# A two-layer decoder trunk on one core: ones matmuls ahead of the first weights, full-width norm sums, outputs on two queues

## The chip, the cores and the metric

The kernel runs on one core of a Trainium2 chip. A core has a matrix engine (TensorE, "PE" in the profile, with its weight loads as "PEld"), a vector engine (VectorE, "DVE"), an activation engine (ScalarE, "ACT"), GpSimd ("POOL") and SyncE ("SP"), which here only issues transfers. SyncE and ScalarE each have a queue of transfers; 16 DMA engines carry them out. The engines run their own instruction streams in order and wait for one another by semaphores. The metric is the device time of one execution in microseconds.

## The reference

Input is x with 256 positions of 2048 features, all in fp32. Each of two layers does:

```
h = rms_norm(x); z = h @ w_in[l]                 # 2048 -> 5120
q, k, v, gu, gv = split(z)                       # 8 heads of 128, 8 gMLP groups of 128
attn = dilated_attention(rotary(q), rotary(k), v)
gm   = gelu(gu) * (tril(w_s) @ layer_norm(gelu(gv)) + b_s)
x = x + concat(attn, gm) @ w_out[l]              # 2048 -> 2048
x = x + square(relu(rms_norm(x) @ w_up[l])) @ w_down[l]   # 2048 -> 8192 -> 2048
```

A last `rms_norm(x, final_g)` follows. `rms_norm` is x times the reciprocal root of (mean of squares + 1e-6), times a gain per feature.

## The kernel before

**Layout.** x stays on chip as 16 chunks of 128 features (partitions) by 256 positions, in the tile `x`. The host hands every weight matrix over in blocks of 128 x 1024 (512 KB), in the order of use.

**Matmuls.** fp32 values are split into a high part (type fp32r, a copy by ScalarE) and a low part (the rest, a subtraction by VectorE), for weights (`hi`, `lo`, lines 118 and 126) and for activations (`hs`, lines 181 and 182). Each product is three matmuls: high by high, low weight by high, high weight by low. `natural` (lines 275 to 294) puts positions on the output's partitions and is used for v and gv; one block is 12 matmuls of 512 columns. `transposed` (lines 242 to 273) puts features there; one block is 24 matmuls of 256 columns, 12 for each of two output chunks, which share one PSUM bank `acc`. Smaller matmuls (scores, transposes, norms) are plain fp32 into banks `aux`.

**Order.** All work is written out by hand as a list of steps, one for each block of weights. Before the matmuls of a step the loop (lines 623 to 642) issues what later blocks need: high parts up to some blocks ahead, then low parts, then the loads of raw weights on SyncE's queue; six raw blocks, seven high and six low ones fit. After a step come its consumer, functions hooked to that step's number, and a queue of attention work. Engines run their instructions in this written order.

**The start** (lines 612 to 621). The gains (`cols`) are issued on ScalarE's queue; ScalarE runs one Tanh, which brings in its function table. SyncE issues x's first two chunks, the first weight block in two halves, the next two chunks of x, the second block, and so on. ScalarE makes the high parts of chunks 0 and 1, then the two high halves of the first block; VectorE the low parts in the same order. The first step is a `natural` one: its matmuls want, in turn, the high weight half, the low weight half, and the low part of chunk 0.

**Norms.** The reciprocal root is applied after the matmul, since it is one number for a position. `square` gathers squares over chunks in the tile `nacc` (the last pair of the last norm stays alone, in `nsq`); `factor` (lines 201 to 209) sums them over partitions with matmuls that use the squares as weights and a column of ones, so that positions land on partitions in a tile of two columns; `rsqrt` (lines 220 to 237) takes the reciprocal root there by a bit trick and three Newton rounds, twelve VectorE instructions; `spread` (lines 210 to 218) brings the row of roots to all partitions with two matmuls by the identity. For the norm ahead of the MLP (`n2`) `factor` is hooked behind the MLP's second step and `spread` behind its third; the first reader is the consumer of the fourth step (line 563).

**The tail.** The last `w_down` steps end with `update` (lines 326 to 337): VectorE adds the result to x, ScalarE squares, and in the last layer ScalarE multiplies x by the final gain. After the last step come `factor`, `spread` without its copy, and for each of eight pairs of chunks a VectorE product with the row of roots, read from PSUM, and a transfer of 256 KB on SyncE's queue (lines 646 to 652).

Of the kernel before, what the change touches and what calls it, by code (L numbers as in the profile page):

```python
# [21 lines left out]
F32 = mybir.dt.float32  # L22
# [3 lines left out]
OP = mybir.AluOpType  # L26
# [25 lines left out]
BUDGET = 1.2  # L52
D_SCORES, D_NORM, D_TURN, D_VALUES = 2, 1, 3, 2
# [21 lines left out]
def trunk(ctx: ExitStack, tc: tile.TileContext, layout, xT, consts, gains, w, b_sp, w_sp, out):  # L75
# [59 lines left out]
    ones = cp.tile([P, P], F32, name="ones")  # L135
    x = cp.tile([P, KC, S], F32, name="x")
# [35 lines left out]
    class Norm:  # L172
# [37 lines left out]
        def spread(self, copy=True):  # L210
            self.ps = aux_bank()
            for tt in range(2):
                pe.matmul(self.ps[:, tt * P:(tt + 1) * P], lhsT=self.r[:, tt:tt + 1].to_broadcast([P, P]), rhs=ident,
                          start=(tt == 0), stop=True, skip_group_check=True)
            if not copy:
                return
            self.R = t32("nR", [S])
            act.activation(self.R, self.ps[:, 0:S], AF.Copy)

    def rsqrt(e, y, src, scale, eps, shape):  # L220

        tag = "x".join(map(str, shape))
        v = t32("rv", shape, tag=f"rv{tag}")
        t = t32("rt", shape, tag=f"rt{tag}")
        vec.tensor_scalar(v, src, scale, eps, op0=OP.mult, op1=OP.add)
        vec.tensor_scalar(t.bitcast(I32), v.bitcast(I32), 1, None, op0=OP.logical_shift_right)
        e.tensor_scalar(y.bitcast(I32), t.bitcast(I32), -1.0, MAGIC, op0=OP.mult, op1=OP.add)
        for _ in range(3):
            if e is vec:
                vec.scalar_tensor_tensor(t, y, -0.5, y, op0=OP.mult, op1=OP.mult)  # L230
                vec.tensor_tensor(t, t, v, op=OP.mult)
                vec.scalar_tensor_tensor(y, t, 1.5, y, op0=OP.add, op1=OP.mult)
# [9 lines left out]
    def transposed(name, l, row0, nk, col0, ncols, moving, after, between=None):  # L242
# [10 lines left out]
        for n, (c, k0) in enumerate(order):  # L253
# [4 lines left out]
            def mm(wt=wt, k0=k0, c=c):  # L258
                if k0 == 0:
                    accs[c] = acc_bank()  # L260
                ps = accs[c]
                for cb in range(2):
                    o = ps[:, cb * S:(cb + 1) * S]
                    for k in range(4):
# [3 lines left out]
                        pe.matmul(o, lhsT=hi, rhs=xs[:, 0, :], start=(k0 + k == 0 and cb == 0), stop=False,  # L268
# [57 lines left out]
    def update(norm, c, ps, final, last):  # L326

        alone = last and c == KC - 2
        for j in range(2) if alone else [slice(0, 2)]:
            xj = x[:, c + j, :] if alone else x[:, c:c + 2, :]  # L330
            vec.tensor_tensor(xj, xj, pair(ps)[:, j, :], op=OP.add)  # L331
# [7 lines left out]
    def layer(l, n1, n2, n3, last):  # L339
# [229 lines left out]
        for e in range(9):  # L569
            if e < 8:  # L570
                transposed("w_up", l, 0, KC, e * 1024, 1024, from_hs, after_up(e))
            if e:
                transposed("w_down", l, (e - 1) * 1024, 8, 0, D, from_tiles([hid[e - 1]], NH),
                           lambda c, ps, e=e: update(n3, c // P, ps, e == 8, last))
        hook(base + 1, n2.factor)
        hook(base + 2, n2.spread)
# [35 lines left out]
    nc.scalar.dma_start(cols, gains)  # L612
    vec.memset(ones, 1.0)
    warm = cp.tile([P, 1], F32, name="warm")
    act.activation(warm, ones[:, 0:1], AF.Tanh)
# [31 lines left out]
    n.factor()  # L647
    n.spread(copy=False)
    ov = out.rearrange("(k p) t -> p k t", p=P)
    for c in range(0, KC, 2):  # L650
        vec.tensor_tensor(x[:, c:c + 2, :], x[:, c:c + 2, :], n.ps[:, None, 0:S].to_broadcast([P, 2, S]), op=OP.mult)  # L651
        nc.sync.dma_start(ov[:, c:c + 2, :], x[:, c:c + 2, :])
# [36 lines left out]
```

## Time and profile before

| | us |
|---|---|
| median of 3 runs (2075.73 to 2076.0) | 2075.97 |
| the profiled execution | 2075.94 |
| its span | 2073.8 |
| TensorE busy | 2056.3 |
| VectorE busy | 1254.5 |
| ScalarE busy | 930.1 |
| GpSimd busy | 68.3 |

The span runs from the first recorded instruction to the last; the execution's own time has some 2 us more around it. In rows of the timeline stand start, duration, engine, line, operation, what is written and read, the count, and the idle time before it with what ended it. In rows of the chain of waits stand start, length and the work that held up what came next. In rows of grouped instructions stand count, busy time, the mean duration in ns, and the idle time before. A row for a window has the busy time of each engine, then granted TensorE clock, DMA share and GB/s. Times inside the profile count from the span's start.

### The profile page before, as it was taken

How to read it: one execution, taken by the hardware profiler on the slowest of the kernel's cores; microseconds unless marked ns; L12 is line 12 of the kernel's file. 1: busy time of each engine (PE TensorE's matmuls, PEld its weight loads, DVE VectorE, ACT ScalarE, POOL GpSimd, SP SyncE). 2: the span in 40 equal slices, each digit the busy share in tenths (PEclk: the TensorE clock that was granted, in tenths of full speed). 3: DMA queues.
4: the chain of work that ended last, by engine and by line, in shares of the span. 5: the costliest groups of instructions: out<-in, count | busy, mean ns of one | idle time of the engine just before them, and what ended most of it. 6: DMA issues, size and time to landing. Idle time of an engine off the chain costs nothing.

```text
span 2073.8 us, 40168 instructions
## 1 busy us (share of the span) xinstructions
PE 2056.3 (99%) x17212; PEld 2019.2 (97%) x17212; DVE 1254.5 (60%) x1502; ACT 930.1 (45%) x1128; POOL 68.3 (3%) x90
## 2 busy tenths in 40 slices
PE   8999999999999999999999999999999999999997
PEld 7998999999999999999989989999999999999997
DVE  7566766656565655655756666665565555555555
ACT  6555444344343443434545554543344434434333
POOL 0002300000000000000000032000000000000000
PEclk9999999999999999999999999999999999999998
DMA  8544555555565556655564455555655656556562
GB/s 309 190 163 165 189 191 188 203 192 186 192 204 192 194 184 203 197 188 202 187 215 162 164 183 183 194 182 204 204 183 186 202 199 200 187 186 201 189 201 82
DMA packets 111523, 395.36 MB, mean 191 GB/s; under 512 B 12272, under 2 KB 16368, under 8 KB 111344
## 3 DMA queue, kind: packets, MB, share of 16 engines
q1 hardware_dynamic: 110480, 390.12, 56.5%
q8 instruction: 134, 2.20, 0.4%
q10 hardware_dynamic: 864, 2.68, 0.3%
q14 instruction: 45, 0.37, 0.1%
HBM read 390.65 MB, written 2.10 MB: 189 GB/s over the span
## 4 chain that ended last, share of the span: by engine, by line
PE 99%; DVE 0%; DMA 0%; ACT 0%; issue 0%; DVEq 0%; ACTq 0%
PE acc L268 29%; PE acc L270 29%; PE acc L272 29%; PE acc L291 3%; PE acc L293 3%; PE acc L292 3%; PE aux L505 0%; PE aux L449 0%; PE aux L409 0%; PE aux L438 0%; DVE x L651 0%; PE aux L206 0%; PE aux L412 0%; PE aux L451 0%; PE aux L359 0%; DMA x<-in_xT 0%
## 5 line engine op out<-in xcount | busy, mean ns | idle before, releaser
L118 ACT ACTIVATE hi<-raw 128x1024 fp32r<-128x1024 f32 (+1 forms) x737 | 754.9, 1053 | 455.4 <-PE acc L272 374.9
L126 DVE TENSOR_TENSOR lo<-raw,hi 128x1024 fp32r<-128x1024 f32 (+1 forms) x737 | 864.2, 1218 | 54.2 <-ACT hi L118 26.3
L268 PE MATMUL acc<-hs,hi 128*128 128x256 f32 x2816 | 781.5, 278 | 0.0
L272 PE MATMUL acc<-hs,hi 128*128 128x256 f32 x2816 | 778.8, 277 | 0.0
L270 PE MATMUL acc<-hs,lo 128*128 128x256 f32 x2816 | 778.8, 277 | 0.0
L268 PE MATMUL acc<-half,hi 128*128 128x256 f32 x2560 | 706.7, 276 | 0.0
L272 PE MATMUL acc<-half,hi 128*128 128x256 f32 x2560 | 706.6, 276 | 0.0
L270 PE MATMUL acc<-half,lo 128*128 128x256 f32 x2560 | 706.6, 276 | 0.0
L268 PEld LDWEIGHTS acc<-hs,hi 128*128 128x128 f32 x2816 | 529.9, 188 | 0.4 <-issue 0.2
L270 PEld LDWEIGHTS acc<-hs,lo 128*128 128x128 f32 x2816 | 528.8, 188 | 0.4 <-issue 0.2
L272 PEld LDWEIGHTS acc<-hs,hi 128*128 128x128 f32 x2816 | 528.6, 188 | 0.0
L270 PEld LDWEIGHTS acc<-half,lo 128*128 128x128 f32 x2560 | 480.6, 188 | 0.0
L268 PEld LDWEIGHTS acc<-half,hi 128*128 128x128 f32 x2560 | 480.6, 188 | 0.0
L272 PEld LDWEIGHTS acc<-half,hi 128*128 128x128 f32 x2560 | 480.6, 188 | 0.0
L331 DVE TENSOR_TENSOR x<-x,acc 128x512 f32<-128x512 f32 (+1 forms) x152 | 99.6, 660 | 319.2 <-PE acc L272 319.2
L459 ACT ACTIVATE half<-mz 128x512 fp32r<-128x512 f32 x64 | 40.6, 634 | 364.6 <-DVE mz L564 364.6
L563 DVE TENSOR_TENSOR mz<-acc,nR 128x512 f32<-128x512 f32 x64 | 44.3, 692 | 230.7 <-PE acc L272 230.7
L291 PE MATMUL acc<-hi,hs 128*128 128x512 f32 x256 | 102.8, 402 | 5.4 <-ACT hi L118 5.4
L293 PE MATMUL acc<-hi,hs 128*128 128x512 f32 x256 | 101.3, 396 | 0.0
L292 PE MATMUL acc<-lo,hs 128*128 128x512 f32 x256 | 100.9, 394 | 0.0
L181 ACT ACTIVATE hs<-x,cols 128x256 fp32r<-128x256 f32 x64 | 29.1, 501 | 96.4 <-DVE x L331 94.8
L460 DVE TENSOR_TENSOR half<-mz,half 128x512 fp32r<-128x512 f32 x64 | 44.3, 692 | 44.8 <-ACT half L459 44.8
(90 smaller groups left out, 680.2 us busy)
## 6 DMA issues: line engine op xcount, KB each, us to landing
raw<-in_w SPq DMA_DIRECT2D x735, 512.0 KB, 4.4
x<-in_xT SPq DMA_DIRECT2D x8, 256.0 KB, 7.3
out<-x SPq DMA_DIRECT2D x8, 256.0 KB, 3.0
spb<-in_b_sp ACTq DMA_DIRECT2D x2, 512.0 KB, 7.3
wsp<-in_w_sp ACTq DMA_DIRECT2D x2, 512.0 KB, 9.0
raw<-in_w SPq DMA_DIRECT2D x2, 256.0 KB, 4.0
con<-in_consts ACTq DMA_DIRECT2D x1, 512.0 KB, 6.6
cols<-in_gains ACTq DMA_DIRECT2D x1, 56.0 KB, 2.9
```

The costliest lines, as they stand in the source:

```text
L118: act.activation(self.h[:, j * m:(j + 1) * m], self.raw[:, j * m:(j + 1) * m], AF.Copy)
L126: vec.tensor_tensor(lo[:, r], self.raw[:, r], self.h[:, r].bitcast(F32), op=OP.subtract)
L268: pe.matmul(o, lhsT=hi, rhs=xs[:, 0, :], start=(k0 + k == 0 and cb == 0), stop=False, skip_group_check=True)
L270: pe.matmul(o, lhsT=wt.lo[:, k, cb * P:(cb + 1) * P], rhs=xs[:, 0, :], start=False, stop=False, skip_group_check=True)
L272: pe.matmul(o, lhsT=hi, rhs=xs[:, 1, :], start=False, stop=last, skip_group_check=True)
L291: pe.matmul(ps, lhsT=xh, rhs=hi, start=(k0 + k == 0), stop=False)
L292: pe.matmul(ps, lhsT=xh, rhs=lo, start=False, stop=False)
L293: pe.matmul(ps, lhsT=xl, rhs=hi, start=False, stop=(k0 + k == KC - 1))
L331: vec.tensor_tensor(xj, xj, pair(ps)[:, j, :], op=OP.add)
L459: act.activation(t[:, c:c + 2, 0, :], src, AF.Copy)
L460: vec.tensor_tensor(t[:, c:c + 2, 1, :], src, t[:, c:c + 2, 0, :].bitcast(F32), op=OP.subtract)
L563: vec.tensor_tensor(z, pair(ps), n2.R[:, None, :].to_broadcast([P, 2, S]), op=OP.mult)
```

## The change

*Start.* x's first two chunks go on ScalarE's queue, followed there by the gains; all other loads stay on SyncE's. The second weight block is loaded, and both first blocks are split, in two halves. Nine fp32 matmuls of ones by ones into a spare bank are written ahead of all other TensorE work. The parts of the first chunks are interleaved with those of the weights: chunk 0, both high halves, chunk 1, both low halves, and the same for the second block.

*Norm ahead of the MLP.* `factor` and `spread` give way to `everywhere`: two fp32 matmuls with a full matrix of ones as weights leave the sum on all partitions, and `rsqrt` runs on 128 x 256.

*Last norm.* The last block of the last `w_down` writes its two chunks to two banks, so that the add of the first can begin ahead of the second's matmuls. Four matmuls on ones sum the squares; ScalarE takes a root with Sqrt (its table is asked for by a small Sqrt early in the last MLP), VectorE a reciprocal and one Newton round, and writes the row of roots to PSUM; ScalarE copies it to SBUF for GpSimd.

*Outputs.* GpSimd makes the pairs 10 and 14, VectorE the other six; transfers go alternately on SyncE's and ScalarE's queue.

```
+WARM = 9
@@ Norm
+        def total(self, n0, n1, last):
+            if n0 == 0:
+                self.ps = aux_bank()
+            parts = [a[:, j, :] for a in self.acc for j in range(2)]
+            for n in range(n0, n1):
+                pe.matmul(self.ps[:, 0:S], lhsT=ones, rhs=parts[n], start=(n == 0), stop=(last and n == n1 - 1))
+
+        def everywhere(self):
+            self.total(0, 2, True)
+            self.R = t32("nR", [S])
+            rsqrt(vec, self.R, self.ps[:, 0:S], 1.0 / D, NORM_EPS, [S], tags=("p0", "q"))
+
+        def finish(self):
+            y, v, t = t32("ny", [S], tag="p0"), t32("nv", [S], tag="q"), t32("nt", [S], tag="p1")
+            act.activation(y, self.ps[:, 0:S], AF.Sqrt, bias=eps, scale=1.0 / D)
+            vec.tensor_scalar(v, self.ps[:, 0:S], 1.0 / D, NORM_EPS, op0=OP.mult, op1=OP.add)
+            vec.reciprocal(y, y)
+            vec.scalar_tensor_tensor(t, y, -0.5, y, op0=OP.mult, op1=OP.mult)
+            vec.tensor_tensor(t, t, v, op=OP.mult)
+            vec.scalar_tensor_tensor(self.ps[:, S:2 * S], t, 1.5, y, op0=OP.add, op1=OP.mult)
+            self.R = t32("nR", [S])
+            act.activation(self.R, self.ps[:, S:2 * S], AF.Copy)
@@ transposed (apart: the last block has a bank for each chunk)
+                two = apart and c == ncols - 256
-                    accs[c] = acc_bank()
+                    accs[c] = [acc_bank(), acc_bank()] if two else acc_bank()
-                    o = ps[:, cb * S:(cb + 1) * S]
+                    o = ps[cb][:, 0:S] if two else ps[:, cb * S:(cb + 1) * S]
@@ update
-        alone = last and c == KC - 2
+        alone = last and final and c == KC - 2
-            vec.tensor_tensor(xj, xj, pair(ps)[:, j, :], op=OP.add)
+            vec.tensor_tensor(xj, xj, ps[j][:, 0:S] if alone else pair(ps)[:, j, :], op=OP.add)
@@ layer, MLP
-        hook(base + 1, n2.factor)
-        hook(base + 2, n2.spread)
+        hook(base + 1, n2.everywhere)
+        if last:
+            hook(base + 4, lambda: act.activation(warm, ones[:, 0:1], AF.Sqrt))
@@ load_to
-                nc.sync.dma_start(x[:, c:c + 2, :], xv[:, c:c + 2, :])
+                (nc.scalar if c == 0 else nc.sync).dma_start(x[:, c:c + 2, :], xv[:, c:c + 2, :])
+            if c == 0:
+                nc.scalar.dma_start(cols, gains)
@@ start
-    nc.scalar.dma_start(cols, gains)
     vec.memset(ones, 1.0)
+    vec.memset(eps, NORM_EPS)
+    spare = aux_bank()
+    for _ in range(WARM):
+        pe.matmul(spare[:, 0:P], lhsT=ones, rhs=ones, start=True, stop=True)
+    for i in range(RAW_BUFS):
+        load_to(i + 1, 2 if i < 2 else 1)
     act.activation(warm, ones[:, 0:1], AF.Tanh)
-    for i in range(RAW_BUFS):
-        load_to(i + 1, 2 if i == 0 else 1)
     for i in range(2):
-        norms[0].chunks(2 * i)
-        high_to(i + 1, 2 - i)
-        low_to(i + 1, 2 - i)
+        norms[0].chunks(2 * i, 1)
+        high_to(i + 1, 2)
+        norms[0].chunks(2 * i + 1, 1)
+        low_to(i + 1, 2)
@@ tail
-    n.factor()
-    n.spread(copy=False)
+    n.total(0, 4, True)
+    n.finish()
-    for c in range(0, KC, 2):
-        vec.tensor_tensor(x[:, c:c + 2, :], x[:, c:c + 2, :], n.ps[:, None, 0:S].to_broadcast([P, 2, S]), op=OP.mult)
-        nc.sync.dma_start(ov[:, c:c + 2, :], x[:, c:c + 2, :])
+    def scale(c):
+        e, r = (nc.gpsimd, n.R) if c in (10, 14) else (vec, n.ps[:, S:2 * S])
+        e.tensor_tensor(x[:, c:c + 2, :], x[:, c:c + 2, :], r[:, None, :].to_broadcast([P, 2, S]), op=OP.mult)
+
+    for i, c in enumerate((0, 2, 4, 10, 6, 8, 12, 14)):
+        scale(c)
+        (nc.sync if i % 2 == 0 else nc.scalar).dma_start(ov[:, c:c + 2, :], x[:, c:c + 2, :])
```

More of the change, by code (lines that the diff above doesn't have):

```diff
@@ L135, in trunk @@
     ones = cp.tile([P, P], F32, name="ones")
+    eps = cp.tile([P, 1], F32, name="eps")
+    warm = cp.tile([P, 1], F32, name="warm")
     x = cp.tile([P, KC, S], F32, name="x")
@@ L209, in factor, with spread @@
             rsqrt(vec, self.r, ps[:, 0:2], 1.0 / D, NORM_EPS, [2])
-        def spread(self, copy=True):
+        def spread(self):
             self.ps = aux_bank()
@@ L240, in trunk, with transposed @@
     steps = []
-    def transposed(name, l, row0, nk, col0, ncols, moving, after, between=None):
+    def transposed(name, l, row0, nk, col0, ncols, moving, after, between=None, apart=False):
         order = [(c, k) for c in range(0, ncols, 256) for k in range(0, nk, 4)]
@@ L267, in mm @@
                         last = k0 + k == nk - 1
-                        pe.matmul(o, lhsT=hi, rhs=xs[:, 0, :], start=(k0 + k == 0 and cb == 0), stop=False,
+                        pe.matmul(o, lhsT=hi, rhs=xs[:, 0, :], start=(k0 + k == 0 and (two or cb == 0)), stop=False,
                                   skip_group_check=True)
```

12 lines of the change are left out of this document (5 added, 7 removed).

## The prediction

> **What bounds the kernel now.** I read the page first, the busy times and the chain of waits, then the chain in order of time at both ends, because 99% of it lies on one engine.
>
> ```profile
> span 2073.8 us, 40168 instructions
> PE 2056.3 (99%) x17212; PEld 2019.2 (97%) x17212; DVE 1254.5 (60%) x1502; ACT 930.1 (45%) x1128; POOL 68.3 (3%) x90
> ...
> PE 99%; DVE 0%; DMA 0%; ACT 0%; issue 0%; DVEq 0%; ACTq 0%
> ```
>
> TensorE sets the end. The change leaves its projection matmuls as they are, so only three places can move: the first 11 us, the norm before each MLP (there TensorE itself does other work), and what follows the last projection matmul. The start, in the chain:
>
> ```profile
> 0.74 3.12 DMA x<-in_xT
> ...
> 3.95 0.91 ACT hs L181 x2
> ...
> 5.43 0.79 PE acc L291
> ...
> 9.93 0.43 PE acc L291
> 10.36 0.26 PE acc L292
> 10.62 0.23 PE acc L293
> ```
>
> Until about 10.3 us a matmul takes 0.43 us of the chain, afterwards 0.23: TensorE runs at half speed for its first 4.9 us, although the granted clock of the windows (below) reads 1.00 there. The first block of weights (12 matmuls) ends at 10.85.
>
> The tail, in the chain:
>
> ```profile
> 2058.52 0.13 PE acc L272
> ...
> 2058.67 0.43 DVE x L331
> ...
> 2059.12 0.42 ACT nsq L189
> ...
> 2059.59 1.07 PE aux L206 x8
> ...
> 2060.68 0.17 DVE rv L225
> ...
> 2063.06 1.24 PE aux L213 x4
> ...
> 2064.32 0.69 DVE x L651
> ```
>
> From the last projection matmul (2058.65) to the first scaled pair of chunks (2065.01) pass 6.4 us: residual add, square, sum over partitions into two columns, twelve tiny VectorE steps at 0.198 us each (2060.68 to 2063.06), a matmul pair that spreads the root, the first product. Then only transfers are left:
>
> ```profile
> 2065.04 5.02 SPq L652 DMA_DIRECT2D out<-x  x8
> ```
> ```profile
> 3.00:4.00 1.00, 0.00 (x0) 0.00 (x0) 0.00 (x0) 0.05 (x1) 0.00 (x0) 1.00 1.05 388
> ...
> 2061.00:2062.00 1.00, 0.00 (x0) 0.00 (x0) 0.83 (x6) 0.00 (x0) 0.00 (x0) 0.85 0.02 8
> ...
> 2066.00:2068.00 2.00, 0.00 (x0) 0.00 (x0) 2.00 (x5) 0.00 (x0) 0.00 (x0) 0.50 1.01 341
> ```
>
> In the windows (the last three columns are granted clock, DMA share, GB/s; the first row is from the loads at the start) the 16 engines are full at 341 GB/s while the outputs leave; eight of 256 KB are 2.1 MB, 6.2 us, plus about 2.5 us of start and landing, is the 8.76 us from first issue to the end of the span. VectorE and the issues pace a pair at 0.63 us (5.02 / 8), the engines take 0.77 for one.
>
> **Part 1: the tail.** Prices:
>
> ```profile
> L331 DVE TENSOR_TENSOR x<-x,acc 128x256 f32<-128x256 f32 x16 | 6.0, 418 | 20.7 <-PE acc L272 20.7
> L409 PE MATMUL aux<-k,q 128*128 128x256 f32 x32 | 8.2, 378 | 0.0
> L218 ACT ACTIVATE nR<-aux 128x256 f32<-128x256 f32 x4 | 1.5, 383 | 14.0 <-PE aux L213 14.0
> L427 DVE RECIPROCAL den<-den 128x4 f32<-128x4 f32 x8 | 1.4, 178 | 0.2
> L232 DVE SCALAR_TENSOR_TENSOR nr<-rt,nr 128x2 f32<-128x2 f32 x15 | 2.4, 161 | 0.5
> L351 POOL TENSOR_TENSOR wsp<-wsp,con 128x1024 f32<-128x1024 f32 x2 | 5.3, 2630 | 842.5 <-DMA wsp<-in_w_sp 842.5
> L615 ACT ACT_TABLE_LOAD x1 | 1.3, 1283 | 1.2 <-PEq L672 1.2
> ```
> ```profile
> 2059.78 0.89 ACT L199 ACTIVATE x<-x,cols 128x256 f32<-128x256 f32 x2
> ```
> ```profile
> 82.53 0.86 PE aux L409 x4
> ...
> 341.11 0.79 PE aux L206 x8
> ...
> 344.83 0.44 PE aux L213 x4
> ```
>
> An fp32 matmul leaves two records (L409 issues 16 and has 32), so 256 columns cost 0.43 (0.86 / 2).
>
> *Two banks for the last pair.* The add of chunk 14 no longer waits for the twelve matmuls of chunk 15 (12 x 0.114 = 1.4 us). Only chunk 15 stays on the path: add 2058.67 to 2059.10, square to 2059.54.
>
> *The sum.* Four fp32 matmuls of 256 columns in order: two on the accumulator and one on chunk 14 end at 2058.65 + 1.29 = 2059.94, later than the square; the fourth at 2060.37, its end 0.16 later (378 against a spacing of 215 ns): 2060.53. This takes the place of L206's end at 2060.66, and no spread follows.
>
> *The root.* ScalarE is in order: behind the square stand two gain multiplies (L199, 0.89 us) until 2060.4, just hidden by the sum. Sqrt by L218: 2060.55 to 2060.95. VectorE's mean-plus-eps runs beside it. Then four VectorE steps in a row on 256 columns (reciprocal, three of Newton). By L331 one is 0.42, with the 0.037 between dependent steps (0.198 against L232's 0.161) 0.46. The reciprocal is unseen at this width: at four columns it takes 178 ns where other steps take 161. If those 17 ns are fixed, it is 0.46; if they are per column (4.2 ns each), 256 columns cost 0.42 + 1.08 = 1.5. I take 0.46, since the only row says little more than "one more VectorE step", and keep 1.5 for the range. Root done at 2060.95 + 4 x 0.46 = 2062.8, first product at 2063.5, first output 2063.52. Gain 1.52; with the dear reciprocal 0.48.
>
> [...]
>
> *The outputs.* Two queues feed the same full engines: 0. The second queue's issue is hidden by the 0.77 us that each transfer takes. If a second queue let the engines write at the 388 GB/s of the loads, 2.1 MB would take 0.75 us less (range). GpSimd's two pairs, at half of L351 about 1.3 us each, start when ScalarE's copy of the root is there (2063.2), so pair 10 is ready at 2064.5 and pair 14 at 2065.8; the engines want them as fourth and last, at 2066.9 or later. Without that cover one of them late costs 0.5.
>
> *The table.* Tanh, Exp, Square and Copy all run on the one table load of 1.28 us. Sqrt is new; its load is asked for early in the last MLP, where ScalarE is under half busy and weights are prepared four blocks (11 us) ahead: 0. If Square or Copy needed the old table back, a load would fall between the last square and Sqrt: 1.3.
>
> **Part 2: the MLP norm, twice.** On TensorE the factor (0.79) and spread (0.44) give way to two fp32 matmuls of 256 columns (0.86): gain 0.37 each, 0.74 in all, straight off the path. VectorE now does twelve steps at 0.46 instead of 0.2, 3.1 us more, and the ScalarE copy goes. Behind the first of these steps, which waits for the sum, VectorE has the low halves of weights; they are made about five blocks ahead (13.7 us), and the four accumulator banks hold three groups back. VectorE is 60% busy, so it catches up: 0; uncovered it would be 3.1 us each.
>
> **Part 3: the start.** Rows of VectorE and ScalarE there:
>
> ```profile
> 0.73 0.45 ACTq L612 DMA_DIRECT2D cols<-in_gains  x1
> ...
> 4.49 0.88 DVE L182 SCALAR_TENSOR_TENSOR hs<-x,cols,hs 128x256 fp32r<-128x256 f32 x2 [3.49 <-ACT hs L181]
> 4.76 0.61 ACT L118 ACTIVATE hi<-raw 128x512 fp32r<-128x512 f32 x1
> ...
> 5.41 0.69 DVE L126 TENSOR_TENSOR lo<-raw,hi 128x512 fp32r<-128x512 f32 x1
> ...
> 6.60 0.63 ACT L118 ACTIVATE hi<-raw 128x512 fp32r<-128x512 f32 x1 [1.22 <-DMA raw<-in_w]
> ...
> 8.59 1.06 ACT L118 ACTIVATE hi<-raw 128x1024 fp32r<-128x1024 f32 x1 [0.41 <-DMA raw<-in_w]
> ...
> 11.73 1.23 DVE L126 TENSOR_TENSOR lo<-raw,hi 128x1024 fp32r<-128x1024 f32 x1
> ...
> 13.82 0.39 PE L292 MATMUL acc<-lo,hs 128*128 128x512 f32 x1
> ```
> ```profile
> cols<-in_gains ACTq DMA_DIRECT2D x1, 56.0 KB, 2.9
> ```
>
> If nine fp32 matmuls on ones (two passes of 128 columns, 0.11 us warm by L213, twice that slow: 9 x 0.44 = 4 us, about 1.1 to 5.1) bring the clock up, the first block shrinks from 5.4 us to 12 x 0.23 = 2.8. But operands set that stage then, and the new order makes them later. ScalarE now has hs 0, both high halves, then hs 1; VectorE has hs-low 0, hs-low 1, then the low halves. So the first low half, which the second matmul needs, waits for hs-low 1, that for hs 1, that for the second high half, that for its weights. From the time T at which x and the gains are there: 0.46 + 0.61 + 0.61 + 0.46 + 0.44 + 0.69 = T + 3.27, against T + 2.15 now (3.95 to 6.10).
>
> T itself: x and then the gains go on ScalarE's queue, the gains issued at 1.18 instead of 0.73. Lower bound 1.18 + 2.9 (their landing time now, 0.73 to about 3.6) = 4.1; upper, if x shares the engines with both 256 KB weight halves ahead of it, 3.86 + 512 KB / 388 GB/s = 5.2, with the gains 5.4. I take 4.7. The second block's weights come in two transfers instead of one, an issue more on SyncE (0.4), which runs ahead of the engines: 0. The second matmul then starts at 8.0, the second block at 10.5; its weights still land near 8.59, so high half 9.2, hs 3 9.65, hs-low 3 10.1, low halves 10.8 and 11.5, two more hs-lows and the third block's low part at 13.6. The third block's second matmul goes at 13.6 instead of 13.82: gain 0.2. If the second weight half lands at 6.6 as now, the second matmul waits until 8.8 and the third block is 0.45 later than now. I take 0 between them. Even with no such stall the third block's low part was ready only at 12.96 (11.73 + 1.23): the start can gain at most 13.82 - 12.96 = 0.9.
>
> **The sum.** 2075.94 (the profiled execution's own time, 2073.8 of span and 2.1 around it) - 1.52 - 0.74 - 0 = 2073.7. Its own time stands 0.03 below the median of 2075.97, so the forecast against that is the same.
>
> **Rivals.**
>
> *The clock is lost again: slower.* At the tail the granted clock falls from 1 to 0.5 inside the row 2061 to 2062 (mean 0.85, so near 2061.7), 3 us after the last projection matmul, though one-column matmuls ran until 2060.65; and at the start 4.9 us of matmuls passed before the speed rose (5.43 to about 10.3). In the new start TensorE has one real matmul between about 5.1 and 8.0. If the clock isn't raised by then, or is lost in this gap, the slow 4.9 us begin anew at the second matmul. At 8.0 they last to 12.9 and cover 11.4 matmuls; the other 11.6 up to the third block end at 15.6 instead of 13.6 (13.82 - 0.23): loss 2.0. With the late weight half they last from 8.8 to 13.7, and the third block begins at 16.4: loss 2.8, 2076.5. It decides the sign from a loss above 2.26, that is, if the second matmul comes after 8.3. Against it: the matmuls on ones are four microseconds of full work.
>
> [...]
>
> *The dear reciprocal:* 1.04 less gain, 2074.7. For it the 17 ns, against it that they may be fixed.
>
> *The start gains all that operands allow:* 0.9 more, 2072.8, if low halves come earlier than the written order says.
>
> *The outputs leave faster on two queues:* 0.75 more, 2072.9; against it stands the DMA share of 1.01.
>
> *A table load before Sqrt:* 2075.0.
>
> **How the numbers follow.** The forecast 0.42, the dear reciprocal 0.20, the clock 0.20, the start 0.08, the outputs 0.05, the table 0.05. Range: the two best cases reach 2072.8 and 2072.9, together 2072.0; the lost clock reaches 2076.5, with the dear reciprocal 2077.5. I take 2072.2 to 2076.6. A measurement of this kernel tells about 0.2% (4.2 us) from no change, and every case lies inside that: the gains together (1.52 + 0.74 + 0.9 + 0.75 = 3.9) don't reach it, nor do the losses together (1.04 + 2.8 + 1.3 = 5.1, less the 2.26). So same 0.94, and 0.03 on each side for what I haven't seen.
>
> **What would show it.** The first output issue 8.76 us before the end and about 1.5 us nearer to the last projection matmul than now; one VectorE reciprocal of 0.42 us, or of 1.5; the MLP norms' two matmuls at 0.86; the second real matmul at 8 to 8.8 us, released by the low half, and spacings of 0.23 from there. Wrong I am if the second matmul starts before 7, if spacings of 0.43 are seen past 11 us, or if the output phase is shorter than 8 us.

## The result, and the profile after

The changed kernel takes 2130.01 us (median of 5 runs, 2129.28 to 2130.41), the kernel before in the same series 2075.75 (2075.58 to 2076.0): a ratio of 1.0261 [1.0249, 1.0272]. It is 54 us slower where 2.3 us less was forecast. The profiled execution took 2130.33 us itself.

The page of the changed kernel, busy times:

```profile
span 2128.5 us, 40136 instructions
...
PE 2111.1 (99%) x17202; PEld 2073.3 (97%) x17202; DVE 1260.0 (59%) x1488; ACT 930.3 (44%) x1131; POOL 70.4 (3%) x92
```

TensorE still sets the end and is busy 55 us longer, with ten matmul records fewer. It isn't waiting either. These are all the waits of TensorE in the changed kernel (what waited, for whom; us in total, times, longest):

```profile
PE acc L321 <- ACT hi L119: 1.3, 1, 1.3
PE acc L322 <- DVE lo L127: 1.2, 1, 1.2
PE aux L649 <- DVE eps L646: 1.1, 1, 1.1
```

3.6 us, all at the start. The 55 us must lie in the matmuls themselves. Windows of 200 us inside the two MLPs, first of the kernel before, then of the changed one (length and sum; busy time and records of TensorE, its weight loads, VectorE, ScalarE, GpSimd; granted clock, DMA share, GB/s):

```profile
400.00:600.00 200.00, 200.00 (x1767) 200.00 (x1766) 115.11 (x120) 79.75 (x83) 0.00 (x0) 1.00 0.59 196
1600.00:1800.00 200.00, 200.00 (x1767) 200.00 (x1766) 115.56 (x123) 80.50 (x84) 0.00 (x0) 1.00 0.58 195
```
```profile
400.00:600.00 200.00, 200.00 (x1700) 200.00 (x1699) 110.74 (x116) 75.95 (x79) 0.00 (x0) 1.00 0.58 190
1600.00:1800.00 200.00, 200.00 (x1700) 200.00 (x1699) 111.46 (x116) 77.46 (x79) 0.00 (x0) 1.00 0.57 186
```

TensorE is full in both, the granted clock is 1.00 in both, but the same stream of matmuls comes out 1,700 times instead of 1,767. A record (0.28 us) lasts longer than the distance to the next, so about two in each window reach over its edges: 200 / 1,765 = 0.1133 us a matmul before, 200 / 1,698 = 0.1178 after. An MLP has 256 blocks of 24 matmuls, all but two of them behind its norm: 254 x 24 = 6,096; 12,192 in both layers by 4.45 ns are 54 us. Taken from the starts of all the matmuls behind the norm, the mean distance is 113.3 ns before and 117.8 ns after, in both MLPs.

Both paces were in the profile of before. Two windows of its attention part, full of the same matmuls:

```profile
86.00:94.00 8.00, 8.00 (x70) 8.00 (x69) 4.84 (x7) 7.23 (x14) 0.00 (x0) 1.00 0.44 152
203.00:211.00 8.00, 8.00 (x73) 8.00 (x72) 7.68 (x17) 5.14 (x6) 3.27 (x2) 1.00 0.41 129
```

With the same two taken off, 8 / 68 = 0.118 and 8 / 71 = 0.113, at a granted clock of 1.00 both times. The first follows the matmuls of the attention scores, and the pace holds at least until the next group of small matmuls.

The three places that the prediction spoke of. The start in the chain of the changed kernel, and rows of its timeline, with the matmul that opens the third block in each kernel (the changed one, then the one before):

```profile
1.23 4.12 DMA cols<-in_gains
...
5.44 0.51 ACT hs L184
...
8.56 0.80 PE acc L322
```
```profile
1.05 4.21 PE L649 MATMUL aux<-ones 128*128 128x128 f32 x18 [1.05 <-DVE eps L646]
6.52 0.80 PE L321 MATMUL acc<-hi,hs 128*128 128x512 f32 x1 [1.26 <-ACT hi L119]
...
13.42 0.47 PE L321 MATMUL acc<-hi,hs 128*128 128x512 f32 x1
13.73 0.39 PE L322 MATMUL acc<-lo,hs 128*128 128x512 f32 x1
...
16.24 0.39 PE L321 MATMUL acc<-hi,hs 128*128 128x512 f32 x1
```
```profile
13.60 0.39 PE L291 MATMUL acc<-hi,hs 128*128 128x512 f32 x1
```

The gains are there at 5.35, the second matmul goes at 8.56, matmuls run at half speed until about 13.5 although ones filled 1.05 to 5.26 (the matmul behind them, at 6.52, takes 0.80 like the one at 8.56), and the third block begins at 16.24 instead of 13.60: 2.64 us lost.

The norm ahead of the MLP, in the chain, as predicted:

```profile
343.16 0.86 PE aux L228 x4
```

The tail, in the chain:

```profile
2112.77 0.12 PE acc L302
2112.89 1.74 PE aux L228 x8
...
2114.65 0.48 ACT ny L239
...
2115.16 0.42 DVE nv L240
2115.58 1.67 DVE ny L241
...
2118.66 0.39 ACT nR L246
...
2119.08 0.69 DVE x L689
```
```profile
2119.79 3.50 SPq L693 DMA_DIRECT2D out<-x  x4
2120.40 2.99 ACTq L693 DMA_DIRECT2D out<-x  x4
```

From the last projection matmul's end (2112.89) to the first output issue (2119.79) pass 6.90 us; before it was 6.39 (2058.65 to 2065.04). From there to the end of the span 8.71 us, against 8.76.

One more part moved. Counted from the starts, 864 matmuls of the attention parts ran at the slow pace before and 480 in the changed kernel (from 100 to 300 us of the span there are 1,534 matmul records before, 1,542 after): 384 by 4.45 ns are 1.7 us gained. With 2.64 lost at the start, 0.51 in the tail and 0.37 gained in each MLP norm (0.86 instead of 0.79 + 0.44), the parts give 54.2 - 1.7 + 2.4 = 54.9 us, against 54.4 between the two profiled executions.

### The profile page after: what moved, and what is told of

Read it like the earlier page. It is cut to its first block, busy times and chain, and to the rows that moved or that the text cites. A ratio compares the mean times of both kernels' runs of the same rounds, so it can differ in the third digit from the quotient of the medians.

```text
span 2128.5 us, 40136 instructions
## 1 busy us (share of the span) xinstructions
PE 2111.1 (99%) x17202; PEld 2073.3 (97%) x17202; DVE 1260.0 (59%) x1488; ACT 930.3 (44%) x1131; POOL 70.4 (3%) x92
## 4 chain that ended last, share of the span: by engine, by line
PE 99%; DVE 0%; DMA 0%; ACT 0%; issue 0%; DVEq 0%; ACTq 0%
PE acc L300 30%; PE acc L298 29%; PE acc L302 29%; PE acc L321 3%; PE acc L323 3%; PE acc L322 3%; PE aux L535 0%; PE aux L479 0%; PE aux L439 0%; PE aux L468 0%; DMA cols<-in_gains 0%; PE aux L442 0%; PE aux L481 0%; PE aux L228 0%; PE aux L389 0%; DVE x L689 0%
## 5 line engine op out<-in xcount | busy, mean ns | idle before, releaser
L298 PE MATMUL acc<-hs,hi 128*128 128x256 f32 x2816 | 790.9, 281 | 0.0
L302 PE MATMUL acc<-hs,hi 128*128 128x256 f32 x2816 | 788.2, 280 | 0.0
L300 PE MATMUL acc<-hs,lo 128*128 128x256 f32 x2816 | 788.2, 280 | 0.0
L298 PE MATMUL acc<-half,hi 128*128 128x256 f32 x2560 | 717.0, 280 | 0.0
L302 PE MATMUL acc<-half,hi 128*128 128x256 f32 x2560 | 716.8, 280 | 0.0
L300 PE MATMUL acc<-half,lo 128*128 128x256 f32 x2560 | 716.8, 280 | 0.0
```

What stands on the lines that cost most here:

```text
L300: pe.matmul(o, lhsT=wt.lo[:, k, cb * P:(cb + 1) * P], rhs=xs[:, 0, :], start=False, stop=False, skip_group_check=True)
L302: pe.matmul(o, lhsT=hi, rhs=xs[:, 1, :], start=False, stop=last, skip_group_check=True)
```

## The experiments

### What slows the MLP

Three candidates: VectorE, which has twelve wide steps more, starves TensorE (V); the wide sums themselves set the stream behind them to the slow pace (P); or it takes the wide sums together with the tiles' new places (Q): `eps` and `warm` now stand ahead of `x`, where the kernel before had `warm` behind it, so that every tile behind `x` lies 32 bytes further on in its partition. (A one-column tile takes 32 bytes, not the eight of which the expectations speak: the built program of the changed kernel has `eps` at byte 21,568 and `warm` at 21,600, and `hs` at 117,056 where the kernel before has it at 117,024. Places are those of the programs; no profile shows them.) V has already lost its ground, as TensorE waits for nothing in the MLP.

**e1, the changed kernel with the old MLP norm.**

```
-        hook(base + 1, n2.everywhere)
+        hook(base + 1, n2.factor)
+        hook(base + 2, n2.spread)
```

> The changed kernel with the norm ahead of the MLP put back to factor and spread; start, tail and outputs stay changed. Theory P (pace): the fp32 group that stands at the MLP's entry sets the spacing of the 6,096 matmuls behind it, 0.113 us after spread and 0.118 after the two wide sums, until the next fp32 group. Then both MLPs go back to 0.113 and the time to 2130.0 - 2 x 26.5 + 0.74 = 2077.7 us. Theory S (storage): the two new one-column tiles ahead of x move every later tile by 8 bytes and reads become slower; then nothing changes but the 0.74: 2130.7 us. Theory V (VectorE): the twelve full-width steps delay the weights: then PE waits would show, and at most 3.1 us for each norm would come back: 2124 us.

2076.54 us (10 runs), ratio to before 1.0005 [0.9995, 1.0014]. The 53 us are gone. All the rest of the change stays, and costs 0.6 us by the medians, which is inside the interval; the 1.7 us that the attention part gains are in that.

**e2, the kernel before with the wide sums alone.** `total`, `everywhere` and `rsqrt` at [S] as in the change, hooked in place of `factor` and `spread`.

> The kernel before with only the norm ahead of the MLP changed to the two wide sums and twelve full-width steps. Theory P: 2075.8 - 0.7 + 53 = 2128 us, spacing 0.118 in both MLPs. Theory S: 2075.1 us, spacing 0.113. Theory V: up to 2082 us, with waits of TensorE in the profile.

2074.46 us, ratio 0.9993 [0.9983, 1.0002]. So the wide sums alone don't do it, and P falls; V falls with it, since VectorE's twelve wide steps are in e2 too.

**e3, the kernel before with the shift alone.**

```
     ones = cp.tile([P, P], F32, name="ones")
+    eps = cp.tile([P, 1], F32, name="eps")
+    warm = cp.tile([P, 1], F32, name="warm")
     x = cp.tile([P, KC, S], F32, name="x")
```

> The kernel before with the two one-column tiles allocated ahead of x (every later tile 8 bytes further) and one memset more, nothing else. Theory P: 2075.8 us, spacing 0.113 in the MLPs. Theory S: about 2128 us, spacing 0.118.

2074.15 us, ratio 0.9992 [0.9982, 1.0001]; MLPs at the fast pace. But the shift isn't without effect. The same window behind the attention scores, in e3:

```profile
86.00:94.00 8.00, 8.00 (x73) 8.00 (x72) 4.84 (x8) 7.59 (x18) 0.00 (x0) 1.00 0.57 192
```

73 instead of 70: there the shift gives the fast pace.

**e5, the kernel before with both**, e2 and e3 in one.

> The kernel before with both: the wide sums ahead of the MLP, and the two one-column tiles ahead of x. A one-column tile takes 32 bytes of a partition, so weights, activations and squares then start at multiples of 64 bytes, as in the changed kernel, and no longer 32 bytes beside them. Theory Q (both together): the wide sums leave the slow pace only with this placement: 0.118 us in both MLPs, 2074.2 + 53 = 2127 us. If neither of them nor both suffice (another part of the change is needed, such as the shifted turn of the aux banks): 2073 us.

2127.61 us (4 runs), ratio 1.025 [1.0235, 1.0265]. Windows of e2, then of e5:

```profile
400.00:600.00 200.00, 200.00 (x1767) 200.00 (x1766) 115.41 (x121) 80.44 (x84) 0.00 (x0) 1.00 0.59 195
```
```profile
400.00:600.00 200.00, 200.00 (x1700) 200.00 (x1699) 110.19 (x116) 77.14 (x80) 0.00 (x0) 1.00 0.56 187
```

Q holds: neither part is slow, both together are, and nothing else of the change is needed.

**e6 and e7, the changed kernel with more padding** ahead of `x`: 32 bytes (e6), 64 bytes (e7).

```
+    pad = cp.tile([P, 1], F32, name="pad")      (e7: [P, 16])
+    vec.memset(pad, 0.0)
```

> The changed kernel with one more one-column tile ahead of x, so that every later tile stands 32 bytes beside multiples of 64 again, as before the change; one memset more. Theory Q: both MLPs at 0.113 us, 2076.5 - 0.74 = 2075.8 us. If the placement is not what the wide sums need: 2130 us.

> As the run with 32 bytes, but the tile more has 16 columns, 64 bytes: every later tile is moved, yet stands at multiples of 64 as in the changed kernel. Theory Q in the form that the place within 64 bytes counts: slow, 2130 us. If it is the absolute place, or chance: 2076 us.

e6: 2130.7 us, ratio 1.0265 [1.0248, 1.0282], its MLPs at the slow pace. e7: 2075.8 us in one run, its MLPs at 1,767 records in 200 us, the fast pace. Both came out against the expectation that multiples of 64 bytes are slow. Counted from the kernel before, with wide sums, a shift of 0 is fast, 32 and 64 are slow, 96 is fast again. So one tile of 64 bytes takes the MLPs' loss away, with the computation unchanged.

**e4 and e8, sums in halves in layer 0; in layer 1 wide sums followed by two matmuls of 128 columns on ones.** e4 stands on the places of the kernel before, e8 on those of the changed kernel. The sums in halves:

```
-            self.total(0, 2, True)
+            for n in range(2):
+                for tt in range(2):
+                    pe.matmul(self.ps[:, tt * P:(tt + 1) * P], lhsT=ones, rhs=parts[n][:, tt * P:(tt + 1) * P],
+                              start=(n == 0 and tt == 0), stop=(n == 1), skip_group_check=True)
```

> As the run with only the wide sums, but in layer 0 each sum is taken in two halves of 128 columns (four fp32 matmuls), and in layer 1 the two wide sums are followed by two fp32 matmuls of ones by ones with 128 columns into a spare bank. Theory P in the form that the width of the last fp32 matmuls decides (128 columns as in spread: fast): both MLPs at 0.113 us, 2075.8 us. P in the form that the wide sums always leave the slow pace, whatever follows at once: layer 0 fast, layer 1 slow, 2102 us. P in the form that only a pause between sum and spread helps: both slow, 2128 us.

> The changed kernel with its placement, but in layer 0 each sum ahead of the MLP is taken in two halves of 128 columns (four fp32 matmuls), and in layer 1 the two wide sums are followed by two fp32 matmuls of ones by ones with 128 columns into a spare bank. If the width of the last fp32 matmuls decides in this placement: both MLPs at 0.113 us, 2077 us. If any wide sum here leaves the slow pace whatever follows at once: layer 0 fast, layer 1 slow, 2103 us. If every fp32 group that reads the squares here does: both slow, 2130 us.

In e4 (2287.7 us) the granted clock was 0.85 over the whole run; there 40 us of the first MLP (from 360) have 321 records, 40 / 319 = 0.1254 us a matmul, and 10 us have 82 in the attention part (from 1200 and 1400) as in the second MLP (from 1700), so that the two paces can't be told apart. In e8, 2102.86 us, the layers differ:

```profile
400.00:600.00 200.00, 200.00 (x1767) 200.00 (x1766) 114.57 (x120) 79.49 (x82) 0.00 (x0) 1.00 0.58 197
1600.00:1800.00 200.00, 200.00 (x1701) 200.00 (x1700) 112.99 (x117) 79.34 (x82) 0.00 (x0) 1.00 0.55 184
```

Sums 128 columns wide left the fast pace behind (1,767 records), sums 256 wide the slow one (1,701), in one program at one set of places; and two small matmuls right behind didn't undo it.

### Whose place is it

The wide sums read the squares (`nacc`) as the moving operand and `ones`, which never moved, as weights; the slowed matmuls read `hi` and `lo` as weights and `hs` or `half` as the moving operand. Theory N: the place of the squares decides. Theory W: that of the weights and activations. e13 and e14 stand on the kernel before with the wide sums, e15 on the changed kernel, e16 again on the former.

```
e13, e15:
-    ... else t32("nacc", [2, S])
+    ... else t32("nacc", [2 * S + 32])[:, 8:8 + 2 * S].rearrange("p (a b) -> p a b", a=2)      (e15: 16 for 8)
e14:
+    pad = tp.tile([P, 8], F32, name="pad")       (tp holds half, nacc and the small tiles, behind hs)
e16:
+    pad = wp.tile([P, 32], F32, name="pad")      (wp holds the weights; all but ones, con and x lie behind it)
```

> The kernel before with the wide sums, no shift of the weights or activations; the tile of the squares is 128 bytes larger and the sums read it from 32 bytes in, so that the squares alone lie 32 bytes later (the tiles behind them 128 bytes later). Theory N (the place of the squares, which the wide sums read, picks the pace): MLP matmuls at 0.1176 us, 2127 us. Theory W (the place of the weight and activation parts, which the projections read, picks it): 0.1132 us, 2074.5 us.

> The kernel before with the wide sums; the weights and the activations' parts (hi, lo, hs) stay in place, while all later tiles (the squares, half, q, k, v, the roots) lie 32 bytes later. Theory N: 0.1176 us, 2127 us. Theory W: 0.1132 us, 2074.5 us, or slow in the down projection alone (half is moved), 2101 us.

> The changed kernel whole, but the squares are read 64 bytes further in a tile 128 bytes larger: 96 bytes later than in the kernel before, where a shift of everything gave the fast pace; weights and activations stay 32 bytes later. Theory N: 0.1132 us, 2076 us. Theory W: 0.1176 us, 2130 us.

> The kernel before with the wide sums and everything from the weights on 128 bytes later. If the pace goes by the place within 128 bytes: 0.1132 us, 2074.5 us, like no shift. If it goes by the absolute place, nothing is known and 2127 us is as likely.

One run each: 2106.95, 2109.06, 2116.91 and 2072.73 us. e16, as fast as without a shift, fits a rule by the place within 128 bytes. The other three lie between the two answers. Windows of e13, each inside a stretch of matmuls that all read `half` (first and third) or all read `hs` (second and fourth):

```profile
435.00:465.00 30.00, 30.00 (x257) 30.00 (x256) 14.79 (x15) 11.55 (x11) 0.00 (x0) 1.00 0.62 197
480.00:510.00 30.00, 30.00 (x267) 30.00 (x266) 18.27 (x20) 12.85 (x15) 0.00 (x0) 1.00 0.47 160
525.00:555.00 30.00, 30.00 (x257) 30.00 (x256) 15.11 (x16) 10.92 (x11) 0.00 (x0) 1.00 0.62 196
570.00:600.00 30.00, 30.00 (x267) 30.00 (x266) 19.52 (x21) 13.64 (x15) 0.00 (x0) 1.00 0.49 164
```

The pace changes at every switch between `hs` and `half`, within one MLP, with no sum in between: 30 / 255 = 0.1178 us on `half`, 30 / 265 = 0.1133 on `hs`. What e13 to e15 have in common is that `half` no longer lies 73,728 bytes behind `hs` as in the kernel before. That suggested a theory S: the pace is picked anew wherever the stream switches between operands, by their places to one another, and a norm's sum is only one such switch. It can be tried without the change.

**e17 and e18, the kernel before with only the pad behind `hs`**, 128 and 32 bytes, no wide sums.

> The kernel before without any part of the change; only the tiles behind hs (half, the squares and all small ones) lie 128 bytes later, as half did in e13. Theory S (what feeds the stream is switched between hs and half, and a switch over a distance other than the 73,728 bytes of the kernel before picks the pace anew, wide sums or not): projections on half at 0.1178 us, on hs at 0.1133, so 2106 to 2109 us. Theory W with wide sums as the only trigger: 0.1133 us throughout, 2076 us.

> The same with 32 bytes instead of 128, as in e14. Theory S: projections on half at 0.1183 us, on hs at 0.1133, 2108 to 2110 us. Theory W with wide sums as the only trigger: 0.1133 us throughout, 2076 us.

2110.06 and 2117.19 us, against 2075.97 for the kernel before. The first two of these windows in e17:

```profile
435.00:465.00 30.00, 30.00 (x258) 30.00 (x256) 16.14 (x17) 11.11 (x11) 0.00 (x0) 1.00 0.59 191
480.00:510.00 30.00, 30.00 (x267) 30.00 (x266) 16.88 (x19) 12.03 (x14) 0.00 (x0) 1.00 0.50 173
```

S holds in its main point: an unused tile of 128 bytes makes the kernel before 34 us slower (one run, borne out by the count of its records). All projections on `half` are 7,680 matmuls (three lines of 2,560); by 4.45 ns that is 34.2 us. e18 came out above its expectation (2108 to 2110) since it also has a slow stretch behind the norm. The runs with narrow or with wide sums together, places in bytes against the kernel before, paces in us from the windows or from the starts of the matmuls in MLP 0:

| | norm's sum | weights, hs | squares | half minus hs | hs behind the norm | half | hs later |
|---|---|---|---|---|---|---|---|
| before | narrow | 0 | 0 | 73,728 | .1133 | .1133 | .1133 |
| e2 | wide | 0 | 0 | 73,728 | .1133 | .1133 | .1133 |
| e1, e3 | narrow | 32 | 32 | 73,728 | .1133 | .1133 | .1133 |
| changed, e5 | wide | 32 | 32 | 73,728 | .1178 | .1178 | .1178 |
| e6 | wide | 64 | 64 | 73,728 | .1178 | .1178 | .1178 |
| e7 | wide | 96 | 96 | 73,728 | .1133 | .1133 | .1133 |
| e16 | wide | 128 | 128 | 73,728 | .1133 | .1133 | .1133 |
| e13 | wide | 0 | 32 | 73,856 | .1133 | .1178 | .1133 |
| e14 | wide | 0 | 32 | 73,760 | .1133 | .1183 | .1133 |
| e15 | wide | 32 | 96 | 73,856 | .1178 | .1178 | .1133 |
| e17 | narrow | 0 | 128 | 73,856 | .1133 | .1178 | .1133 |
| e18 | narrow | 0 | 32 | 73,760 | .1178 | .1183 | .1133 |

Three readings. Behind wide sums the first stretch goes by the place of weights and `hs` and not by that of the squares (e13 and e14 against e2; e15 against e7): N falls. With the distance of before, a switch between `hs` and `half` kept whichever pace there was (.1133 throughout in e2, .1178 in e5); with another distance it set one within the MLP (.1178 on `half` and .1133 on `hs` in e13); the 48 matmuls on `hs` ahead of the norm, behind the output projection on `half`, do not fit in (slow in e14, e17 and e18, not in e13 and e15). And the place alone doesn't fix the pace: in e15 the same matmuls on `hs` run at .1178 first and at .1133 later, so the stream seems to keep a state between switches. What that state is, and the rule by which a switch sets it, stays open, and so does whether the weights' place or that of `hs` counts, since no run moves one without the other; e18 shows that the slow pace can stand behind a narrow sum too (.1178).

### The start and the tail by themselves

These four have the sums in halves, so that the MLPs run at the fast pace. **e9** also has the start put back whole, without ones; **e10** is e9 with ten matmuls on ones ahead of it; **e12** has the new start without the ones; **e11** is e10 with another last norm:

```
e11, in finish (four parts summed into two columns as in factor):
+            vec.tensor_scalar(v, ps[:, 0:2], 1.0 / D, NORM_EPS, op0=OP.mult, op1=OP.add)
+            act.activation(y, v, AF.Sqrt)
             vec.reciprocal(y, y)
             vec.scalar_tensor_tensor(t, y, -0.5, y, op0=OP.mult, op1=OP.mult)
             vec.tensor_tensor(t, t, v, op=OP.mult)
+            vec.scalar_tensor_tensor(y, t, 1.5, y, op0=OP.add, op1=OP.mult)
+            for tt in range(2):
+                pe.matmul(self.ps[:, tt * P:(tt + 1) * P], lhsT=y[:, tt:tt + 1].to_broadcast([P, P]), rhs=ident,
+                          start=(tt == 0), stop=True, skip_group_check=True)
...
+        vec.tensor_tensor(x[:, c:c + 2, :], x[:, c:c + 2, :], n.ps[:, None, 0:S].to_broadcast([P, 2, S]), op=OP.mult)
```

> The changed kernel with two edits: each sum ahead of both MLPs in two halves of 128 columns (both MLPs should then run at 0.113 us, as layer 0 did in the run with halves and ones: 2102.9 - 26.5 = 2076.4 us), and the start put back whole: gains on ScalarE's queue, x on SyncE's, chunks 0 and 1 ahead of the weights, no ones. Theory C (the new start loses 2.5 us because the second matmul waits for the low half and the clock rises only at 13.5): 2073.9 us, clock rise near 10.3. If the new start costs nothing: 2076.4 us.

> As the run with the old start, with ten fp32 matmuls of ones by ones ahead of TensorE's work, nothing else: the ones without the later operands. Theory C, with the clock raised by any busy stretch: matmuls of the first block at 0.23 us from about 6.9 on, gain up to 0.9, 2073.0 to 2073.6 us. If matmuls on ones do not count for the clock: rise near 10.3 as without them, 2073.9 us.

> The changed kernel with the sums in halves and its new start, but without the nine matmuls on ones. If the ones did nothing in that order: the clock rises near 13.5 as with them, 2076.4 us. If they did bring the clock up for part of the time: a later rise, 2077 us or more. If they hold something up: less than 2076 us.

> As the run with the ones only, but the last norm sums into two columns as before the change, takes the root there (VectorE's mean plus eps, ScalarE's Sqrt, a reciprocal and one Newton round, all on 128 x 2) and spreads it with the old matmul pair; two banks for the last pair and outputs on two queues stay, VectorE makes all eight products. Theory R (the tail lost its gain to a reciprocal of 1.7 us on 256 columns and to two waits for ScalarE's reads of the same bank, 0.4 each): the first output goes out some 4.4 us after the last projection matmul instead of 6.9, 2.5 us less than the run with the ones only: 2070.5 to 2071.1 us. If the wide root was no worse than a narrow one: no change.

On one chip, 11 runs each, before 2075.93: e9 2073.47 (ratio 0.9989 [0.998, 0.9998]), e10 2073.06 (0.9987 [0.9979, 0.9996]), e12 2076.31 (1.0002 [0.9993, 1.0011]), e11 2070.73 (0.9976 [0.9967, 0.9985]).

*The start.* The new order costs 2076.31 - 2073.47 = 2.8 us. The ones gain 0.4 in the old order by the medians (e10), though the runs of e9 and e10 overlap. In the new order no gain is shown: with them e7 took 2075.8 in one run and e1 2076.54, but both differ from e12 in other things too. Rows of e10, then of e12:

```profile
5.58 0.80 PE L326 MATMUL acc<-hi,hs 128*128 128x512 f32 x1
6.30 0.64 PE L327 MATMUL acc<-lo,hs 128*128 128x512 f32 x1
6.78 0.39 PE L328 MATMUL acc<-hi,hs 128*128 128x512 f32 x1
...
10.32 0.50 PE L327 MATMUL acc<-lo,hs 128*128 128x512 f32 x1 [0.76 <-DVE lo L127]
```
```profile
6.66 0.79 PE L326 MATMUL acc<-hi,hs 128*128 128x512 f32 x1 [6.66 <-ACT hi L119]
8.70 0.79 PE L327 MATMUL acc<-lo,hs 128*128 128x512 f32 x1 [1.25 <-DVE lo L127]
...
14.41 0.47 PE L328 MATMUL acc<-hi,hs 128*128 128x512 f32 x1
```

In e10 there is no gap between the ones and the weights' matmuls, and full speed (0.39) is there at 6.8; the gain is then lost in waiting for the second block's low part at 10.32. In the new order the second matmul itself comes 2.4 us later than in e10, and full speed at 14.4 without ones. With them it comes at 13.5 in the changed kernel, at 11.6 in e8 and not before 11.4 in e1, whose starts are the same. Rows of e1, and a window of it:

```profile
6.59 0.50 PE L321 MATMUL acc<-hi,hs 128*128 128x512 f32 x1 [1.55 <-ACT hi L119]
8.63 0.79 PE L322 MATMUL acc<-lo,hs 128*128 128x512 f32 x1 [1.54 <-DVE lo L127]
```
```profile
8.10:11.40 3.30, 2.77 (x7) 2.19 (x8) 3.30 (x7) 3.04 (x6) 0.00 (x0) 0.50 1.02 389
```

In e1 the ones had raised the clock: the matmul behind them takes 0.50 us, and 0.80 in the changed kernel. The gap then cost it again, and the granted clock is 0.50 up to 11.4. e8 shows the same rise and fall (0.51 us at 6.80, 0.79 at 8.85); the changed kernel shows no rise ahead of the gap (0.80 at 6.52). So with one and the same start it varied between the profiled executions whether the ones raised the clock, and in none of these three did it last over the gap. (In the traces of the kernel before and of the changed one the records of the granted clock begin with the rise, at 10.3 and 13.6. Windows ahead of that read 1.00 for want of a record, which is why the half speed at the start, 0.43 us a matmul instead of 0.23, doesn't show there.)

From the first matmul without a gap behind it to full speed pass 4.9 us in the changed kernel (8.56 to 13.5) and 5.7 in e12 (8.70 to 14.4), but 3.4 in e9 (5.48 to 8.9) and 2.7 in e8 (8.85 to 11.6). What sets the moment is not shown.

*The tail.* The chain of e11:

```profile
2056.31 1.69 PE aux L247 x16
2058.03 0.17 DVE rv L250
...
2058.22 0.21 ACT nr L251
...
2058.46 0.18 DVE nr L252
...
2059.27 0.72 PE aux L258 x4
...
2060.01 0.69 DVE x L697
```

The reciprocal on two columns takes 0.18 us instead of 1.67 on 256, and the first issue follows 4.42 us after the last projection matmul (2056.31 to 2060.73) instead of 6.90. VectorE makes all eight products there. e11 is 2.3 us faster than e10, so it was the width that cost. Against the 6.39 us of the kernel before, these 4.42 are 0.3 shorter ahead of the root (two banks for the last pair), 1.1 in the root, and 0.5 behind it, where the spreading matmuls take 0.72 instead of 1.24: the granted clock falls at 2061.7 in the kernel before, ahead of them (0.50 from 2062 to 2065); for e11 no window covers them, and the first behind them, from 2062, reads 0.50. Of the 5.2 us that e11 is faster than the kernel before, 1.7 are the attention parts' pace (480 slow matmuls here too).

## Why the prediction was wrong

**The step that failed** is in the prediction's first part: "The change leaves its projection matmuls as they are, so only three places can move". They were left as written, but not as timed. The 54 us are 12,192 MLP matmuls at 0.1178 us instead of 0.1133 (what else moved nearly cancels out), and no bound in the sum covered it: the range ended at 2076.6. Two things had to come together, the wide sums and a shift of 32 bytes that came from two new one-column tiles (e5), and neither alone would have shown (e2, e3). The profile of before held the warning in its windows (70 against 73 records in 8 us at a granted clock of 1.00); I had read the MLP's one pace as the pace.

**Outside of that** the sum missed too. With the fast pace (e7) the changed kernel takes 2075.8, e1 2076.5, where the forecast was 2073.7; that lies near the rival of the lost clock (2076.5), but in part by luck. The start and the tail as measured, less the 0.74 of the norms, would give 2078.3; e7's attention parts have 384 slow matmuls instead of 864, and these 2.1 us were no term of the sum.

*Part 3, the start: the rival's case.* T was 5.44, just above the upper bound of 5.4, where 4.7 was taken. The second matmul came at T + 3.12 (3.27 predicted), inside "8.0 to 8.8". From there half speed lasted 4.9 us, as the rival had it: third block at 16.24 (16.4 in the rival with the late weight half), loss 2.64 (2.8). I had given it 0.20, since the ones "are four microseconds of full work". In the changed kernel's profiled execution they did not raise the clock at all (0.80 us for the matmul behind them), and in e1 they did (0.50) and the gap undid it (0.79 for the next); the rival had named both ways.

*Part 1, the tail: gain 1.52 predicted, loss 0.5 measured.* The mechanisms were right up to the sum: 1.74 us from the last projection matmul (1.88 predicted), Sqrt right behind it. Three terms of the root were mis-sized. The reciprocal took 1.67 us, not 0.46: the dear case, above its bound of 1.5. Mean-plus-eps did not run beside Sqrt but behind it (0.44): both read the same PSUM bank, and so do ScalarE's copy of the root and VectorE's first product (0.43). The rows of waits show VectorE waiting for ScalarE:

```profile
DVE nv L240 <- ACT ny L239: 1.8, 1, 1.8
DVE x L689 <- ACT nR L246: 0.5, 1, 0.5
```

No run here has the two engines on different banks, so whether the bank is the cause is not shown. 1.21 + 0.44 + 0.43 less 0.14 for the sum is the 2.0 between 4.87 and 6.90, within rounding and Sqrt's 0.07.

*The outputs: as predicted.* 8.71 us from the first issue to the end, 8.76 before; two queues moved no more than one did (339 GB/s, 341 before):

```profile
2122.00:2124.00 2.00, 0.00 (x0) 0.00 (x0) 0.75 (x2) 0.00 (x0) 0.00 (x0) 0.50 1.02 339
```

No table load fell into the tail.

*Part 2, the MLP norm: as predicted in itself.* 0.86 us for the sums in both layers, VectorE's extra steps hidden. What followed was not.

## What to carry to other kernels

Before a change is costed, measure the steady spacing of the main loop's matmuls in several places: here one and the same matmul showed two paces, 0.1133 and 0.1178 us, at a granted clock of 1.00, and edits that left the loop alone moved it from one to the other: an unused tile (e17), or wide sums together with a shift of 32 bytes (e5). When a time moves by a per cent or more and no wait explains it, count matmuls per window first, and try an unused tile of 32 to 128 bytes. Where matmuls on ones are to bring the clock up, look for a gap between them and the first real ones: without one full speed came at 6.8 (e10), with one it was lost again (e1, 0.50 up to 11.4). Put a reciprocal on few columns where the layout allows it (0.18 us on 2, 1.67 on 256), and where two engines are meant to work side by side, look in the trace whether they wait for one another (here 0.44 and 0.43 us, both times where they read one PSUM bank).

## What the runs showed of the hardware that I had not expected

- Streams of fp32r matmuls 256 columns wide, each with its own weights, ran at two steady paces, 0.1133 and 0.1178 us (0.1183 on `half` in e14 and e18), at the same granted clock of 1.00. In e13 the pace changed at every switch between `hs` and `half`; in the changed kernel one pace was kept for hundreds of microseconds (1,700 records in each 200 us from 400 to 1000).
- It went by where tiles lie: with wide sums, shifts of 0, 96 and 128 bytes gave 0.1133 us, 32 and 64 gave 0.1178. An unused tile made the kernel before 34 (128 bytes) and 41 us (32 bytes) slower; the kernel before was in a lucky place.
- An effect of a microsecond or two was not clean across kernels whose tiles lie differently: e3, which computes nothing else than the kernel before, took 1.8 us less by the medians (its interval just reaches 1). The pace accounts for 1.7 of it: 480 slow matmuls in its attention parts instead of 864.
- Nine matmuls on ones (4.2 us) ahead of a gap raised the granted clock in the profiled executions of e1 and e8 (0.50 and 0.51 us for the matmul behind them) and not in that of the changed kernel (0.80), and it was at half again behind the gap (e1: 0.50 from 8.1 to 11.4).
- VectorE's reciprocal took 1.67 to 1.74 us on 128 x 256, where a multiplication took 0.42 (changed kernel, e10), and 0.17 on 128 x 2 (e11).
